# A two-layer decoder trunk: earlier loads of the second layer's operands, a mix by broadcast factors, and a gate stage that frees its banks before the exponentials

## The chip, the core and the metric

The kernel runs on one core of one Trainium2 chip. The metric is the time of one execution on the device, in microseconds (us); less is better. An execution with a hardware profile gives the trace on which everything below rests. TensorE is called PE, VectorE DVE, ScalarE ACT, GpSimd POOL; SP is SyncE, which here only issues DMA transfers. PEld is TensorE's loading of weights.

## The reference, cut to what matters

A trunk of two residual layers over 2048 tokens of width 1024. Both layers project the normalised input, compute a mixer output of 768 columns and a memory attention of 256 columns (4 heads against 256 memory tokens), multiply both by a gate and project back:

```python
for i in range(2):
    h = rmsnorm(x, norm_w[i])
    mix, q_mem, gate = gla_mixer(...) if i == 0 else dilated_mixer(...)
    mem_o = memory_attention(q_mem, mem_n, w_memkv[i])
    branch = concatenate([mix, mem_o], axis=-1) * silu(gate)
    x = x + branch @ w_out[i]
return rmsnorm(x, final_norm_w)

def dilated_mixer(h, w_in):          # 6 heads of 128 columns
    for g, (window, dil) in enumerate(((128, 1), (512, 4), (2048, 16))):
        q, k, v = split((h @ w_in[:, g's columns]))
        o, lse = dilated_group(rope(q), rope(k), v, window, dil)
    wts = softmax(stack(lses), axis=0)     # over the three groups
    o = einsum('gbth,gbthd->bthd', wts, stack(outs))
    q_mem, gate = split(h @ w_in[:, the rest], [256])
```

Everything is float32 at the interface. The kernel multiplies in float16 with a high and a low part of each operand, three matmuls for one product.

## The kernel before, in words

**Layer 1** (0 to about 982 us) is gated linear attention in two passes. The second pass walks over 16 blocks of 128 tokens in pairs (m, m + 8): queries, gate, memory attention, output projection (`a2_out`, 24 matmuls of 128x256 for each quarter), the norm of the next layer (`a2_norm`), and for each pair `a2_pair`.

**The seven products.** Layer 2 projects by a fast matrix multiplication: a 2x2 split of a product into seven products instead of eight. Its left operands, sums and differences of quarters of the normalised input, are made by `a2_pair`: `put` (near L880) splits one operand into a high and a low float16 part, SP transposes it by DMA (L890), and it stays in SBUF (operands 0 to 4 of the first half of the tokens, pool h2p) or is stored to DRAM (L892, nine tensors h2d) to be loaded later. Layer 2 uses the operands in the order `OPS = (0, 4, 1, 5, 3, 2, 6)`. `load_h2` (L1013 to 1027) loads the nine stored ones at the start of layer 2: operands 5 and 6 of the first half into wo0 and wo1, then all seven of the second half into wo2, wo3 and the pool wp. They are 128 x 4096 float16, 1 MB each.

**A half.** `sw_half` (L1040) computes 1024 tokens of 256 columns of a projection as seven products of 48 matmuls of 128x128 into two banks ps_mm and one ps_x. A product waits for its weight operand and its input operand; after it, `snap` copies, L1085 adds on DVE and a `fin` given by the caller uses the result. The bank is given back (`rel`) by the `fin` of its last product.

**Weights.** `weights` makes seven operands of a set of 256 columns: a raw 1 MB load into the single buffer stg (L974), per operand one ACT copy (L990) and one DVE step for the low part (L992), and four POOL subtractions (L998). The operands live in eight buffers wq.

**Order of the work.** From layer 2 on, the order on every engine is decided while the program is built. Each piece of work is a Python generator that yields an engine with an estimated time, a wait for an event or a semaphore; a planner (`Flow`) plays them against each other, and instructions are emitted in the order in which the planner lets them go. A changed estimate or condition therefore moves instructions on all engines. On the chip, each engine runs its instructions strictly in that order.

**The mix.** `combos` (L1572 to 1670) does the softmax-weighted sum over the three groups. It runs three times, for a pair of heads each: twice amid layer 2 (near 1600 to 1760 and 2040 to 2160 us) and once in the gate stage. There are 24 items of 128x512 in each run, and each item costs four DVE operations of 128x128 with a per-token scalar: L1655 for the first group of a sum, L1657 for the two that are added to it.

**The gate stage** (`last_stage`, L1779; 2319 to 2580 us) computes the gate's four sets of 256 columns in two halves each, and the second layer's memory attention between them. `gate_fin` takes a result from the bank or from a copy cx: the stored mix is fetched (L1807), the exponent's argument is made on DVE (L1818) or POOL (L1821), ACT does exp, ln and exp (L1824, L1826, L1828), POOL multiplies by the mix or by the memory output OM (L1832, L1835), and DVE multiplies by the gate's own input (L1844), which is the step that frees the bank. The result goes to DRAM (brd). The sets run as (set, half) = (0,0), (0,1), (1,0), (1,1), (3,0), (2,0), (2,1), (3,1); the weights of set 3 are made twice.

**The rows** (`Rows`, L2033 to 2150; from 2580 us) are the output projection of 16 blocks: load the branch row (L2081, L2083), find its scale (L2094), split it on ACT and DVE (L2101, L2103), transpose it by DMA (L2108), then twice 24 matmuls of 128x512 against the output weights (split on ACT and DVE at L2063, L2065), add, normalise (L2132 to L2147) and store. Before, the weights and the first rows are brought in while the last two gate halves run.

## Time and profile before

| what | us |
|---|---|
| median of 3 runs | 2759.14 |
| lowest and highest | 2752.9, 2767.9 |
| the profiled execution | 2755.03 |
| its span in the trace | 2753.0 |
| mean granted clock of TensorE | 0.96 |
| TensorE busy in 0 to 550 (layer 1, first pass) | 483.73 |
| in 550 to 982 (layer 1, second pass) | 401.12 |
| in 1110 to 2319 (layer 2 up to the gate) | 1145.52 of 1209 |

The rows of the other stretches stand in the prediction. In such a table of windows, each engine has its busy microseconds and, in brackets, its instructions; PEclk is the share of TensorE's full clock that was granted while it worked, and DMA the mean busy share of the 16 DMA engines. A row of waits reads: engine, what the waiting instruction writes, its line, then after the arrow the engine that released it with what it wrote and the line, then the sum in us, how many, the longest. A row of groups reads: line, engine, operation, output and input with their tile names, shape, count; then busy us and the mean ns of one; then the engine's idle us ahead of them with what ended it. A row of a timeline has start, duration and the instruction. Matmuls are pipelined: the spacing of their starts tells their cost.

### The profile page before, as it was taken

To read this page: it belongs to the slowest core of one execution; us is meant where nothing else is said; L and a number is where in the kernel's file an instruction comes from. 1 tells how busy PE (TensorE), PEld (TensorE's weight loads), DVE (VectorE), ACT (ScalarE), POOL (GpSimd) and SP (SyncE) were. 2 spreads that over 40 slices of the span, in tenths; PEclk is the share of its full clock that TensorE was granted. 3 is DMA by queue.
4 is the path that set the end of the run, shared out by engine and by line. 5 is a ranking of instruction groups with operands and counts; after the bars stand their busy time and mean duration, and the time that the engine had idled before them with its cause. 6 is when DMAs were issued, how large, how long until landed. Compare 5 with 4: busy or idle time off the path is not lost. (4 is left out here: it accounts for less than half of the span.)

```text
span 2753.0 us, 58869 instructions
## 1 busy us (share of the span) xinstructions
PE 2491.2 (90%) x23431; PEld 1906.5 (69%) x23431; DVE 1718.0 (62%) x3515; ACT 1339.5 (49%) x2938; POOL 865.6 (31%) x712
## 2 busy tenths in 40 slices
PE   6999889899999857989999899999999997877898
PEld 5888778788888755475858484758484767877544
DVE  6445654565666543656665688666787663888654
ACT  6355654553444333445555454555554554656422
POOL 0000000021112122545453444553545443756300
PEclk9999999999999988999999999999999998988899
DMA  5244892455556764676777789776798767678774
GB/s 191 74 130 147 278 271 85 155 117 120 123 137 159 156 152 160 142 157 168 157 170 154 152 196 227 159 165 152 172 207 215 155 151 162 160 190 209 195 207 126
DMA packets 729495, 454.53 MB, mean 165 GB/s; under 512 B 386514, under 2 KB 677892, under 8 KB 728068
## 3 DMA queue, kind: packets, MB, share of 16 engines
q1 hardware_dynamic: 609412, 421.27, 56.3%
q10 hardware_dynamic: 119808, 29.51, 9.5%
q8 instruction: 183, 3.00, 0.5%
q14 instruction: 92, 0.75, 0.1%
HBM read 246.82 MB, written 134.51 MB: 139 GB/s over the span
## 5 line engine op out<-in xcount | busy, mean ns | idle before, releaser
L275 PE MATMUL ps_mm<-w,hT 128*128 128x256 f16 (+1 forms) x1408 | 393.6, 280 | 23.5 <-ACT v L625 11.6
L276 PE MATMUL ps_mm<-w,hT 128*128 128x256 f16 (+1 forms) x1408 | 392.3, 279 | 0.0
L277 PE MATMUL ps_mm<-w,hT 128*128 128x256 f16 (+1 forms) x1408 | 391.4, 279 | 0.4 <-DVE hT L517 0.4
L277 PEld LDWEIGHTS <-w 128*128 128x128 f16 x2080 | 220.5, 106 | 122.9 <-issue 11.5
L276 PEld LDWEIGHTS <-w 128*128 128x128 f16 x2080 | 220.9, 106 | 112.2 <-issue 16.8
L275 PEld LDWEIGHTS <-w 128*128 128x128 f16 x2080 | 221.0, 106 | 106.4 <-DMA w<-h2d 6.1
L275 PE MATMUL ps_mm<-w,w 128*128 128x128 f16 (+1 forms) x1172 | 262.5, 260 | 6.4 <-ACT p L1069 3.0
L1075 POOL TENSOR_TENSOR u<-u,p 128x512 f32<-128x512 f32 x128 | 176.0, 1375 | 290.1 <-ACT u L1069 284.1
L276 PE MATMUL ps_mm<-w,w 128*128 128x128 f16 (+1 forms) x1172 | 261.8, 259 | 1.3 <-DVE w L992 1.3
L277 PE MATMUL ps_mm<-w,w 128*128 128x128 f16 (+1 forms) x1172 | 261.5, 259 | 0.0
L269 POOL TENSOR_TENSOR stg<-mp,stg 128x512 f16<-128x512 f32 x16 | 18.5, 1156 | 728.9 <-ACT stg L268 725.0
L992 DVE SCALAR_TENSOR_TENSOR w<-stg,wsc,w 128x512 f16<-128x512 f32 x217 | 192.0, 885 | 70.6 <-ACT w L990 70.3
L1471 ACT ACTIVATE pm<-pm,st,qsc 128x256 f32<-128x256 f32 (+1 forms) x288 | 156.9, 545 | 114.9 <-DVE st L1465 103.6
L998 POOL TENSOR_TENSOR stg<-stg 128x512 f32<-128x512 f32 x124 | 170.6, 1376 | 121.9 <-DVE w L992 109.0
L1479 POOL TENSOR_TENSOR ph<-pm,ph 128x512 f16<-128x512 f32 (+2 forms) x144 | 155.7, 1082 | 160.0 <-ACT ph L1477 72.4
L990 ACT ACTIVATE w<-stg,wsc 128x512 f16<-128x512 f32 x217 | 154.3, 714 | 97.3 <-POOL stg L998 26.3
L275 PE MATMUL ps_mm<-w,h 128*128 128x128 f16 x896 | 162.9, 227 | 19.3 <-ACT w L990 11.6
L276 PE MATMUL ps_mm<-w,h 128*128 128x128 f16 x896 | 162.6, 226 | 13.5 <-DVE w L992 13.5
L276 PEld LDWEIGHTS <-hT 128*128 128x128 f16 x1408 | 141.3, 100 | 44.8 <-issue 24.7
L1191 ACT ACTIVATE hl<-cx 128x512 f16<-128x512 f32 x126 | 79.1, 628 | 183.4 <-DVE cx L1085 94.0
L1085 DVE TENSOR_TENSOR cx<-ps_x,u 128x512 f32<-128x512 f32 x128 | 88.0, 688 | 119.8 <-PE ps_x L277 102.6
L277 PE MATMUL ps_mm<-w,h 128*128 128x128 f16 x896 | 162.5, 226 | 0.0
(439 smaller groups left out, 7949.9 us busy)
## 6 DMA issues: line engine op xcount, KB each, us to landing
stg<-in_w_in_b SPq DMA_DIRECT2D x62, 512.0 KB
qkd<-hl SPq DMA_DIRECT2D x144, 192.0 KB
stg<-in_w_in_b SPq DMA_DIRECT2D x72, 256.0 KB
vud<-hl SPq DMA_DIRECT2D x72, 256.0 KB
q<-qkd SPq DMA_DIRECT2D x72, 256.0 KB
od<-cx SPq DMA_DIRECT2D x72, 256.0 KB
fo<-od SPq DMA_DIRECT2D x72, 256.0 KB
x<-in_x SPq DMA_DIRECT2D x32, 512.0 KB
```

Of the source, the lines that this page charges most:

```text
L269: G.tensor_tensor(out=lo, in0=src, in1=hi, op=ALU.subtract)
L275: PE.matmul(o, sh, mh, start=first, stop=False, skip_group_check=free)
L276: PE.matmul(o, sh, ml, start=False, stop=False, skip_group_check=free)
L277: PE.matmul(o, sl, mh, start=False, stop=last, skip_group_check=free)
L990: A.activation(out=t[:, 0], in_=src, func=AF.Copy, scale=s1)
L992: V.scalar_tensor_tensor(out=t[:, 1], in0=src, scalar=s1, in1=t[:, 0], op0=ALU.mult, op1=ALU.subtract)
L998: G.tensor_tensor(out=o_, in0=i0, in1=i1, op=ALU.subtract)
L1075: G.tensor_tensor(out=d, in0=d, in1=sn["p1"], op=ALU.add)
L1085: V.tensor_tensor(out=cv(o), in0=vw(t), in1=cv(sn[tag]), op=ALU.add)
L1191: A.activation(out=hi, in_=src, func=AF.Copy, scale=SQ)
L1471: A.activation(out=p_, in_=p_, func=AF.Exp, scale=sc, bias=st[:, sj[jj]:sj[jj] + 1], accum_out=st[:, 16 + sj[jj]:17 + sj[jj]])
L1479: G.tensor_tensor(out=ph[:, width:2 * width], in0=pm[:, :width], in1=ph[:, :width], op=ALU.subtract)
```

## The change

- **Operands.** h2p now holds operands 0, 4, 1, 5, 3 of the first half, in the order of use. In the last block of layer 1, three of the second half (0, 4, 1) are loaded for 384 of 512 tokens into the wp pool ahead of the block's memory attention, and after the block's output projection operands 2 and 6 of the first half go whole into wo0 and wo1, and 5 and 3 of the second half for 384 tokens into wo2 and wo3. The last pair's transposes fill the remaining 128 tokens in place. `load_h2` is left with operands 2 and 6 of the second half. `a2_norm` writes a tile of its own rather than over its input.
- **Mix.** An item is one 128x512 multiply by factors that are read with a broadcast, on DVE or POOL, whichever has less planned work, and, for two of three groups, one 128x512 add on DVE. In the order that comes out, 25 multiplies stand on DVE (9, 9 and 7 in the three runs) and 47 on POOL (15, 15, 17), with 48 adds on DVE.
- **Gate stage.** The mix or memory output is fetched ahead by a thread of its own; the memory output goes through DRAM (omd). DVE makes the exponent's argument always (now L1845), then multiplies the gate's input into the fetched tile (L1849) and gives the bank back; exp, ln, exp (L1854 to 1858) and POOL's multiply follow. Four weight sets instead of five, the last with six tiles outside wq (three of gx, three of wq2); the halves run (0,0), (0,1), (1,0), (1,1), (2,0), (3,0), (2,1), (3,1).
- **Rows.** They are set up at the start of the gate stage; their weights go into the h2p tiles as the last half-0 products free them, and raw weights and the first two rows into stg and h2_0. The tiles have 256 columns each, so a row is 2 x 48 matmuls of 128x256 rather than 2 x 24 of 128x512. The third row and later ones load into wp, after the last half. All 56 gate products now stand ahead of the first row on TensorE.

The diff, cut to what the text speaks of:

```diff
-    for o in range(5):
-        h2s[0][o] = tl(h2p, [P, 2, 4, 512], F16, f"h2_{o}")
+    OPS = (0, 4, 1, 5, 3, 2, 6)
+    DIRECT, EARLY = (0, 4, 1, 5, 3), (0, 4, 1)
+    for n_, o in enumerate(DIRECT):
+        h2s[0][o] = tl(h2p, [P, 2, 4, 512], F16, f"h2_{n_}")
...
-            V.scalar_tensor_tensor(out=xt, in0=xt, scalar=r, in1=nw1, op0=ALU.mult, op1=ALU.mult)
-            return xt
+            xn = tl(kx, [P, D], F32, "x")
+            V.scalar_tensor_tensor(out=xn, in0=xt, scalar=r, in1=nw1, op0=ALU.mult, op1=ALU.mult)
+            return xn
+
+        def early(o, pl, tag):
+            t = h2s[1][o] = tl(pl, [P, 2, 4, 512], F16, tag)
+            SY.dma_start(t.rearrange("p a k t -> p (a k) t")[:, :, 0:384],
+                         h2_d[o].rearrange("p a k t -> p (a k) t")[:, :, 0:384])
...
             if n == NB - 1:
                 raw0 = load_raw(0, wp, "w")
                 raw1 = load_raw(NJ, wp, "w")
+                for o in EARLY:
+                    early(o, wp, "w")
...
-            xns.append(a2_norm(a2_out(b, bT, it)))
+            xt = a2_out(b, bT, it)
+            if n == NB - 1:
+                for o in (2, 6):
+                    h2s[0][o] = tl(wo01, [P, 2, 4, 512], F16, f"wo{o == 6:d}")
+                    SY.dma_start(h2s[0][o], h2_d[7 + (o == 6)])
+                for o in (5, 3):
+                    early(o, wo23, f"wo{2 + (o == 3)}")
+            xns.append(a2_norm(xt))
...
-        for o in (5, 6):
...
-        yield "t", 12.0
-        for o in OPS:
-            if o in (2, 6):
-                yield "w", raw_free[o == 6]
-            h2s[1][o] = tl(wo23, [P, 2, 4, 512], F16, f"wo{o - 1}") if o in (3, 4) else \
-                tl(wp, [P, 2, 4, 512], F16, "w")
+        for o in (2, 6):
+            yield "w", raw_free[o == 6]
+            h2s[1][o] = tl(wp, [P, 2, 4, 512], F16, "w")
...
-            yield "V", 0.9
-            for f in range(4):
-                fs = slice(f * P, (f + 1) * P)
-                sc_ = F_[:, g * 32 + i * 16 + c * 4 + f:g * 32 + i * 16 + c * 4 + f + 1]
-                if g == 2:
-                    V.tensor_scalar(out=og[:, fs], in0=og[:, fs], scalar1=sc_, scalar2=None, op0=ALU.mult)
-                else:
-                    V.scalar_tensor_tensor(out=acc[:, fs], in0=og[:, fs], scalar=sc_, in1=acc[:, fs], op0=ALU.mult,
-                                           op1=ALU.add)
+            at = g * 32 + i * 16 + c * 4
+            fb = F_[:, at:at + 4].unsqueeze(2).to_broadcast([P, 4, P])
+            o4 = og.rearrange("p (f d) -> p f d", f=4)
+            on_v = fl.load("V") < fl.load("G")
+            yield ("V", 0.85) if on_v else ("G", 1.45)
+            (V if on_v else G).tensor_tensor(out=o4, in0=o4, in1=fb, op=ALU.mult)
+            if g < 2:
+                yield "t", 0.1
+                yield "V", 0.85
+                V.tensor_tensor(out=acc, in0=og, in1=acc, op=ALU.add)
...
+            def fetch(c, ni):
+                yield "w", e_acc[n * 2 + ni][c] if n < 3 else e_OM[c]
+                yield "g", s_gf
+                oc = tl(gb, [P, 512], F32, "fo")
+                yield "S", 0.5
+                if n < 3:
+                    SY.dma_start(oc, acc_d[n * 2 + ni][c])
+                else:
+                    SY.dma_start(oc.rearrange("p (f d) -> p f d", f=4), om_d[c][:, :, ni * P:(ni + 1) * P])
...
+            for ci, ni in ((0, 0), (1, 1), (1, 0), (0, 1)):
+                outs[ni, hf + 2 * ci] = (Ev(), [])
+                fl.spawn(fetch(hf + 2 * ci, ni), 1)
...
             def fin(src, ci, ni, ps, rel):
                 c = hf + 2 * ci
...
                 yield "g", s_e
                 e = tl(ge, [P, 512], F32, "e")
-                if ps or fl.load("V") <= fl.load("G"):
-                    yield "V", 0.65
-                    V.tensor_scalar(out=e, in0=src, scalar1=neg, scalar2=87.0, op0=ALU.mult, op1=ALU.min)
-                else:
-                    yield "G", 1.35
-                    G.tensor_scalar(out=e, in0=src, scalar1=neg, scalar2=87.0, op0=ALU.mult, op1=ALU.min)
+                yield "V", 0.65
+                V.tensor_scalar(out=e, in0=src, scalar1=neg, scalar2=87.0, op0=ALU.mult, op1=ALU.min)
+                yield "w", outs[ni, c][0]
+                oc = outs[ni, c][1][0]
+                yield "V", 0.8
+                V.scalar_tensor_tensor(out=oc, in0=src, scalar=minv if n == 3 else inv, in1=oc, op0=ALU.mult,
+                                       op1=ALU.mult)
                 yield "t", 0.1
+                fl.put(rel)
                 yield "A", 0.6
                 A.activation(out=e, in_=e, func=AF.Exp)
                 yield "A", 0.7
                 A.activation(out=e, in_=e, func=AF.Ln, bias=one1)
                 yield "A", 0.6
                 A.activation(out=e, in_=e, func=AF.Exp, scale=-1.0)
-                yield "w", there
                 yield "G", 1.4
...
+                G.tensor_tensor(out=e, in0=e, in1=oc, op=ALU.mult)
...
-        for m, n, hf, rel in ((0, 0, 0, False), (0, 0, 1, True), (1, 1, 0, False), (1, 1, 1, True), (2, 3, 0, True),
-                              (3, 2, 0, False), (3, 2, 1, True), (4, 3, 1, True)):
...
+        for n, hf in ((0, 0), (0, 1), (1, 0), (1, 1), (2, 0), (3, 0), (2, 1), (3, 1)):
+            yield from sw_half(W[n], hf, False, 1, False, gate_fin(n, hf), late_jobs)
...
-            for q in range(KT):
-                mm3(t, bT[:, 0, q, :], bT[:, 1, q, :], w[:, 0, q, :], w[:, 1, q, :], q == 0, q == KT - 1)
+            for i in range(2):
+                w = self.w[2 * j + i]
+                for q in range(KT):
+                    mm3(t[:, i * 256:(i + 1) * 256], bT[:, 0, q, :], bT[:, 1, q, :], w[:, 0, q, :], w[:, 1, q, :],
+                        q == 0, q == KT - 1)
```

Three places of the order. The first is SP at the end of layer 1 and the start of layer 2: h2d0 to h2d6 are the stored operands 0 to 6 of the second half, h2d7 and h2d8 the two of the first half; wo, w and tq are tiles, stg is the raw projection weight, vud a store of values, x1d a store of the residual. Before:

```order
L890 DMA_TRANSPOSE tq_1596_11409<-stg_1587_11370 128x8x128
L892 DMA h2d6_86_174<-tq_1596_11409 1024x1x128
L1160 DMA mw_1597_11451<-in_mw 128x256
L954 DMA wo0_1599_11455<-h2d7_87_175 128x4096
L954 DMA wo1_1604_11517<-h2d8_88_176 128x4096
L954 DMA vud0_0_125_213<-hl_1610_11629 256x1x512
L974 DMA stg_1617_11795<-in_w_in_b 128x8x128 x2
L954 DMA vud0_1_126_214<-hl_1616_11791 256x1x512
L954 DMA rope0_1621_11855<-in_rope 128x1024
L954 DMA vud0_0_125_213<-hl_1619_11850 256x1x512
L954 DMA w_1625_11878<-h2d0_80_168 128x4096
```

After, the end of layer 1:

```order
L881 DMA w_1595_11257<-h2d4_84_172 128x8x384
L881 DMA w_1596_11259<-h2d1_81_169 128x8x384
L901 DMA h2d6_86_174<-tq_1555_10895 1024x1x128
L870 DMA x1d_37_125<-x_1585_11134 128x1024
L270 DMA_TRANSPOSE mpt_1572_10978<-stg_1573_10981 128x8x128
L861 DMA x_1602_11282<-in_x 128x1024
L896 DMA_TRANSPOSE w_1594_11255<-stg_1613_11403 128x8x128
L896 DMA_TRANSPOSE w_1596_11259<-stg_1613_11403 128x8x128
L943 DMA wo0_1605_11387<-h2d7_87_175 128x4096
L881 DMA wo2_1607_11391<-h2d5_85_173 128x8x384
L943 DMA wo1_1606_11389<-h2d8_88_176 128x4096
L881 DMA wo3_1608_11393<-h2d3_83_171 128x8x384
```

And after, the start of layer 2:

```order
L901 DMA h2d6_86_174<-tq_1618_11433 1024x1x128
L1175 DMA mw_1619_11475<-in_mw 128x256
L973 DMA vud0_0_125_213<-hl_1630_11649 256x1x512
L973 DMA w_1634_11758<-h2d2_82_170 128x4096
L994 DMA stg_1638_11817<-in_w_in_b 128x8x128 x2
L973 DMA vud0_1_126_214<-hl_1637_11813 256x1x512
```

The loads of h2d7 and h2d8 have moved ahead of most of the last pair's transposes, those of operands 4, 1, 5 and 3 of the second half stand in layer 1 with 384 of 512 tokens, ahead of or behind the memory attention's transpose (mpt), and between the first store of vud and the raw weight there is now one whole operand (h2d2) where there was none.

The second is POOL in the first mix: u is an addition for a projection, ph the low part of softmax results that a transpose waits for, stg a subtraction for weight operands, fo an item of the mix and fac its factors. Before:

```order
L1075 TENSOR_TENSOR u_2579_19388<-u_2579_19388,p_2575_19322 128x512
L1075 TENSOR_TENSOR u_2592_19537<-u_2592_19537,p_2575_19322 128x512
L1479 TENSOR_TENSOR ph_19542<-pm_19427,ph_19542 128x512
L998 TENSOR_TENSOR stg_19328<-stg_19328 128x4x128 x2
L1479 TENSOR_TENSOR ph_19694<-pm_19581,ph_19694 128x512
L998 TENSOR_TENSOR stg_19328<-stg_19328 128x4x128
```

After, the same place:

```order
L1494 TENSOR_TENSOR ph_19542<-pm_19429,ph_19542 128x512
L1018 TENSOR_TENSOR stg_19337<-stg_19337 128x4x128 x2
L1494 TENSOR_TENSOR ph_19695<-pm_19583,ph_19695 128x512
L1670 TENSOR_TENSOR fo_19545<-fo_19545,fac_19088 128x512
L1670 TENSOR_TENSOR fo_19689<-fo_19689,fac_19088 128x512
L1018 TENSOR_TENSOR stg_19337<-stg_19337 128x4x128
L1670 TENSOR_TENSOR fo_19786<-fo_19786,fac_19088 128x512
L1086 TENSOR_TENSOR u_2637_19899<-u_2637_19899,p_2627_19773 128x512
```

Three multiplies of the mix stand between the softmax results and the weights, where before only u, ph and stg took turns.

The third is DVE at the end of the gate stage: bh is the low part of a row's operand with the ACT scale stok, cx a result copied out of its bank, e the gate's argument or product, gm, p2e, itok and cj the steps to a row's scale. Before:

```order
L199 RECIPROCAL stok_34192<-itok_34193 128x1
L2097 TENSOR_SCALAR cj_34194<-winv_5408,itok_34193 128x2
L1844 SCALAR_TENSOR_TENSOR e_33912<-cx_33704,winv_5408,e_33912 128x512
L992 SCALAR_TENSOR_TENSOR w_34037<-stg_33071,wsc_5407,w_34037 128x512
L1818 TENSOR_SCALAR e_34214<-cx_34188,wneg_5411 128x512
L2103 SCALAR_TENSOR_TENSOR bh_34211<-bx_34043,stok_34192,bh_34211 128x1024
L1844 SCALAR_TENSOR_TENSOR e_34196<-cx_34177,cols_88,e_34196 128x512
L1085 TENSOR_TENSOR cx_34300<-ps_x_34069,u_4247_33910 128x512
L1818 TENSOR_SCALAR e_34302<-cx_34300,wneg_5411 128x512
L1844 SCALAR_TENSOR_TENSOR e_34214<-cx_34188,cols_88,e_34214 128x512
L1844 SCALAR_TENSOR_TENSOR e_34302<-cx_34300,cols_88,e_34302 128x512
```

After, where bh is written into half of the tile wo:

```order
L1096 TENSOR_TENSOR cx_34079<-ps_mm_33736,p_4277_33787 128x512
L195 TENSOR_SCALAR p2e_34081<-gm_34023 128x1
L196 TENSOR_SCALAR p2e_34081<-p2e_34081 128x1
L198 TENSOR_SCALAR itok_34025<-p2e_34081 128x1
L199 RECIPROCAL stok_34024<-itok_34025 128x1
L2118 TENSOR_SCALAR cj_34026<-winv_5412,itok_34025 128x2
L1096 TENSOR_TENSOR cx_34089<-ps_x_33915,u_4279_33846 128x512
L1845 TENSOR_SCALAR e_34087<-ps_mm_33677,wneg_5415 128x512
L2124 SCALAR_TENSOR_TENSOR wo_4236_33147<-stg_33854,stok_34024,wo_4236_33147 128x1024
```

Before, the low part of a row (L2103) stood ahead of the last gate result (cx_34300); after, the first row's low part (L2124) stands behind the last product's result (cx_34089) and a gate step.

146 lines of the change are left out of this document (68 added, 78 removed).

## The prediction

> **What bounds the kernel now.** I read the page first, then a table of engine time by stretch, then the waits of TensorE in the stretches that the change touches.
>
> ```profile
> span 2753.0 us, 58869 instructions
> PE 2491.2 (90%) x23431; PEld 1906.5 (69%) x23431; DVE 1718.0 (62%) x3515; ACT 1339.5 (49%) x2938; POOL 865.6 (31%) x712
> ```
>
> TensorE is busy for 90% of the span, so everything that can be won without removing products lies in the other 262 us, and in matmuls that run at a lower clock. The change removes no product. The question is therefore where those 262 us sit.
>
> ```profile
> core 0: us, PE busy (x) PEld busy (x) DVE busy (x) ACT busy (x) POOL busy (x), PEclk, DMA share, GB/s
> 982.00:1110.00 128.00, 87.87 (x858) 64.62 (x858) 54.01 (x65) 40.50 (x66) 42.93 (x34) 0.84 0.53 155
> 1600.00:1760.00 160.00, 149.28 (x1517) 104.96 (x1515) 137.12 (x283) 78.39 (x168) 74.78 (x62) 0.98 0.84 200
> 2040.00:2160.00 120.00, 107.89 (x853) 64.76 (x851) 92.91 (x214) 56.98 (x123) 56.09 (x47) 0.97 0.86 197
> 2319.00:2580.00 261.00, 207.37 (x3144) 201.09 (x3142) 198.34 (x348) 155.93 (x332) 164.66 (x111) 0.87 0.72 179
> 2580.00:2745.00 165.00, 165.00 (x767) 74.78 (x765) 87.62 (x148) 42.75 (x77) 1.27 (x1) 1.00 0.65 183
> ```
>
> The five stretches are the start of layer 2, the two mixes inside it, the gate stage and the output rows. TensorE is idle for 40 us in the first, 11 and 12 us in the mixes and 54 us in the gate stage; the granted clock falls only in the first (0.84) and in the gate stage (0.87). The rows are full: 165 of 165 us at clock 1.00, with nothing to win.
>
> **Term A, the start of layer 2.** These are TensorE's waits from 982 to 1110 us, longest first:
>
> ```profile
> PE ps_mm L275 <- DMA wo<-h2d: 11.9, 1, 11.9
> PE ps_x L275 <- DMA wo<-h2d: 9.7, 1, 9.7
> PE ps_mm L275 <- ACT w L990: 8.9, 2, 8.1
> PE ps_x L275 <- DMA w<-h2d: 6.0, 1, 6.0
> ```
>
> Three of the four wait for an operand tile. Each such gap costs a second time, as the matmuls before and after the longest show:
>
> ```profile
> 1000.07 0.22 PE L275 MATMUL ps_mm<-w,h 128*128 128x128 f16 x1
> 1003.03 0.22 PE L277 MATMUL ps_mm<-w,h 128*128 128x128 f16 x1
> 1015.19 0.29 PE L275 MATMUL ps_mm<-w,wo 128*128 128x128 f16 x1 [11.95 <-DMA wo<-h2d]
> 1020.12 0.22 PE L275 MATMUL ps_x<-w,h 128*128 128x128 f16 x1
> ```
>
> Ahead of the gap 53 matmul steps take 2.96 us, 0.056 each, so a product of 48 takes 2.7 us. The 48 behind the gap, from 1015.19 to 1020.12, take 4.9 us: 2.2 us more. Three gaps hold 11.9 + 9.7 + 6.0 = 27.6 us and about 3 x 2.2 = 6.7 us of slow matmuls.
>
> The change loads operands 2 and 6 of the first half before the last pair of blocks is written out, and five of the second half go partly or wholly into place in layer 1. What is late next is the first projection weight: its load now stands behind one 1 MB operand load on SP's queue (the order above). The price of that is read from the issue of the two loads that were late:
>
> ```profile
> 1008.87 1.03 SPq L954 DMA_DIRECT2D wo<-h2d  x2
> ```
>
> The two megabytes had landed by 1015.19, 6.3 us after the issue: 3.2 us for one. Term A is -27.6 - 6.7 + 3.2 = **-31 us**. At best all 40 us of idleness go; at worst only the longest wait goes, with its slow product (-14).
>
> **Term B, layer 1's end.** The three early loads (0.75 MB each) stand on SP ahead of the last memory attention's transposes. By the 3.2 us per megabyte they are worth at most 2.25 x 3.2 = 7 us of lateness. Against it, 24 output matmuls stand ahead of that attention (2.6 us of cover by the 0.109 us spacing under term S). From -2.6 to +7, I take **+3**, since SP's order is strict there. The separate tile for the norm only frees a wait of VectorE; I count it as nothing, hidden by TensorE's own work.
>
> **Term M, the first two mixes.** The waits of TensorE in the first mix (1600 to 1760), then in the second (2040 to 2160):
>
> ```profile
> PE ps_o L1511 <- DMA pt<-ph: 5.3, 3, 2.4
> PE ps_o L1511 <- DVE cx L1526: 4.1, 1, 4.1
> ...
> ```
>
> ```profile
> PE ps_o L1511 <- DMA pt<-ph: 6.4, 5, 4.0
> PE ps_o L1511 <- DVE cx L1526: 4.7, 1, 4.7
> ```
>
> So of 23 us idle, 4.1 + 4.7 = 8.8 are waits for a VectorE eviction, 11.7 wait for transposes. The mix's own prices: POOL's nearest multiply over the whole trace, VectorE's nearest 128x512 operation, the shortest, median and longest of the small mix operation, and the small operations of the third mix (2316 to 2580):
>
> ```profile
> L1075 POOL TENSOR_TENSOR u<-u,p 128x512 f32<-128x512 f32 x128 | 176.0, 1375 | 290.1 <-ACT u L1069 284.1 <-DVE mden L1965 4.0 <-DMA qkd<-hl 1.9
> L1267 DVE TENSOR_TENSOR xr<-xr,cx 128x512 f32<-128x512 f32 x36 | 34.7, 964 | 10.8 <-POOL cx L1263 9.5
> L1657 DVE SCALAR_TENSOR_TENSOR fo<-fo,fac,fo x192: 332/343/1710, 1608.7 to 2498.5; 128x128 f32<-128x128 f32 x192
> L1657 DVE SCALAR_TENSOR_TENSOR fo<-fo,fac,fo 128x128 f32<-128x128 f32 x64 | 34.1, 591 | 4.2 <-DMA fo<-od 4.1
> L1655 DVE TENSOR_SCALAR fo<-fo,fac 128x128 f32<-128x128 f32 x32 | 21.4, 727 | 4.7 <-DMA fo<-od 4.7
> ```
>
> One mix costs VectorE 34.1 + 21.4 = 55.5 us today. After, 9 multiplies and 16 adds of 128x512 stand on VectorE in each of the first two, 25 x 0.964 = 24 us, and 15 multiplies on POOL, 15 x 1.375 = 21 us. So VectorE is freed of some 31 us a mix, and its 8.8 us of waits go; the 11.7 us of transposes stay, eased at most a little. No row shows a broadcast multiply, so the bounds are -23 (all idleness goes) and +41 (each of the 30 POOL multiplies, standing between softmax operations in POOL's order, delays TensorE by its full 1.375). POOL is busy for under half of both stretches, so I take **-10**.
>
> The small operation has a median of 343 ns and a longest of 1710: VectorE is being held up by something. The Trainium skill, page "SBUF — State Buffer", section "Who interferes with whom", says that a VectorE instruction with two SBUF inputs contends with a GpSimd instruction that reads SBUF, and that the later one blocks fully; the trace's spread agrees. By that rule the 41 us of POOL multiplies could hold VectorE's adds as long, and M would be about 0, the sum 2690.
>
> **Term C, the gate stage.** Rows of 2316 to 2580 that the change touches, and TensorE's waits from 2310 to 2600:
>
> ```profile
> L1821 POOL TENSOR_SCALAR e<-cx,wneg 128x512 f32<-128x512 f32 x15 | 34.9, 2329 | 10.1 <-DVE cx L1085 6.2 <-DVE w L992 3.6 <-DMA brd<-e 0.3
> L992 DVE SCALAR_TENSOR_TENSOR w<-stg,wsc,w 128x512 f16<-128x512 f32 x28 | 25.6, 914 | 11.8 <-ACT w L990 11.8
> L998 POOL TENSOR_TENSOR stg<-stg 128x512 f32<-128x512 f32 x16 | 24.1, 1507 | 19.6 <-DVE w L992 19.2
> L1818 DVE TENSOR_SCALAR e<-cx,wneg 128x512 f32<-128x512 f32 x8 | 4.8, 614 | 0.1
> ```
>
> ```profile
> PE ps_mm L276 <- DVE w L992: 15.4, 4, 8.4
> PE ps_mm L275 <- ACT w L990: 7.7, 3, 3.7
> PE ps_mm L275 <- DVE e L1844: 7.6, 2, 5.8
> PE ps_x L276 <- DVE w L992: 5.4, 1, 5.4
> ```
>
> 28.5 us wait for weight operands, and 7.6 for the gate product (L1844) that frees a bank. The change makes four weight sets instead of five, gives the last one further tiles, and multiplies out of the bank before the exponentials rather than after POOL's multiply, so that a bank no longer waits for ACT and POOL. VectorE's work becomes 198.3 - 55.5 (third mix) + 23 x 0.964 = 22.2 (7 multiplies, 16 adds) - 7 x 0.914 = 6.4 (one set fewer) + 15 x 0.614 = 9.2 (POOL's first step, moved over): 168 us. POOL's becomes 164.7 - 34.9 - 4 x 1.507 + 17 x 1.375 = 147. TensorE's is 207.4 x 0.87 = 180 at full clock. The memory output's detour through DRAM adds 16 stores of 128 KB and 8 loads of 256 KB to SP's queue, 4 MB or 13 us by the price under A, asked for a half ahead and so hidden by the products of that half; the output weights' splits lie in this stage already. No engine fills 261 us. VectorE, through which every chain passes, reached 77% in the second mix (92.9 of 120) and 86% in the first (137.1 of 160); 168 us at these shares are 218 and 195. I take 79%, nearer to the present 76%: 212 us, **-49**. The low end is TensorE's 180 at the first mix's 93%: 194. The high end drops only the bank wait, a fifth of the weight waits (5.7) and 7.6 us of slow matmuls behind them: 240.
>
> **Term G, the gap before the first row.** Before, the operands of the first rows were split ahead of the last gate steps, and rows followed products without a gap. Now the low half of row 0 stands on VectorE behind the last product's eviction and one gate step (the order above). How long a transposed operand takes from there:
>
> ```profile
> 2590.88 1.28 DVE L2103 SCALAR_TENSOR_TENSOR bh<-stg,stok,bh 128x1024 f16<-128x1024 f32 x1
> ```
>
> ```profile
> 2596.63 1.15 ACT L2101 ACTIVATE bh<-w,stok 128x1024 f16<-128x1024 f32 x1 [3.92 <-DMA bT<-bh]
> ```
>
> From the end of the split (2592.16) to the tile being free again behind its transpose (2596.63) is 4.5 us. Eviction and gate step are two VectorE operations of about 0.7, so 1.4 + 1.3 + 4.5 = 7.2 us, and the slow clock behind it about 2.2: **+9**. It is 0 if gate steps of an earlier half leave VectorE free sooner, and some 25 if three rows in turn pay the 7.2.
>
> **Term S, the rows' shape.** The 768 matmuls of 128x512 become 1536 of 128x256. The trace has that shape in layer 1's output:
>
> ```profile
> 960.75 0.27 PE L275 MATMUL ps_x<-wo,bT 128*128 128x256 f16 x1
> ...
> 962.93 0.27 PE L277 MATMUL ps_x<-wo,bT 128*128 128x256 f16 x1
> L276 PEld LDWEIGHTS <-bT 128*128 128x128 f16 x768 | 75.8, 99 | 41.4 <-issue 5.1
> ```
>
> Twenty steps take 2.18 us: 0.109. 1536 x 0.109 = 167.4 against 165: **+3**, rounded up, with each 99 ns weight load hidden behind the matmul before.
>
> **Sum.** -31 + 3 - 10 - 49 + 9 + 3 = -75. The profiled execution took 2755.0 us (its span 2753.0), 0.15% under the median of 2759.1; so 2755 - 75 = 2680.
>
> **Rivals.**
> *The gate stage stays bound by its weights.* The waits for w are the largest there and one load buffer still feeds all sets. With 240 us, C is -21: 2708.
> *Everything fits.* Gate stage 195 us and no gap (C -66, G 0): 2654. For it, no engine is over 168 us; against it, the order of the rows.
> *The early loads only collide elsewhere*, so that the change doesn't do what it says at layer 2's start: A -14, B +7, 2701. For it: 2.25 MB ahead of transposes on one queue; against it: 432 us of layer 1 in which to spread them.
> *POOL's multiplies delay the softmax.* M at +41 and the third mix's 17 x 1.375 = 23 on top: 2680 + 51 + 23 = 2754, no change. Against it: POOL's 47% in the mixes.
> *Slower: weight loads no longer hide.* If a 256-column matmul doesn't cover the load for the next, a step is 0.109 + 0.099 and the rows take 1536 x 0.208 = 319 us, S +154: 2831. It decides as soon as the spacing exceeds 0.2 us. Against it stand the twenty steps at 0.109 with a load each. The Trainium skill, page "TensorE: Matmul & The Clock Gate", section "What overlaps and what doesn't", has a weight load overlap matmuls in flight only when the row group differs, which speaks for this rival; the 0.109 us spacing disagrees.
>
> **How the numbers follow.** My forecast gets 0.47, the weights rival 0.17, everything fits 0.13, the collision 0.12, POOL's delay 0.07, the slow rows 0.04. A measurement of this kernel can tell about 0.5% (14 us) from no change. All cases but the last two are faster by more: 0.89, same 0.07, slower 0.04. The range has to leave out those two and reach the others with their bounds: below, 2654 less a further 9 from A's best end and 10 from M's (2635); above, 2708 with the collision's 21 together (2729).
>
> **What would show it.** Right: no wait for an operand from 982 to 1110 and a clock near 1; an eviction wait gone in both mixes; a gate stage of 195 to 220 us with its bank wait gone; one gap of 5 to 12 us before row 0; steps of 0.109 in the rows. Wrong: weight waits of 25 us and more left in the gate stage, POOL's multiplies as what softmax waits for, steps beyond 0.109, or several gaps among the rows.

## The result, and the profile after

The changed kernel took 2738.3 us in the median of 7 runs (2731.7 to 2745.0), the kernel before 2759.1 (2752.9 to 2769.9): a ratio of 0.992, 95% interval 0.9894 to 0.9946. It is faster by 21 us, and 75 were forecast. Its profiled execution, at 2745.0, is the slowest of its seven, and that of before near its fastest, so the two traces lie only 10 us apart: they show where time was won and lost, but their sum is 11 us short of the medians.

The page of the changed kernel, first lines:

```profile
span 2743.0 us, 60361 instructions
PE 2485.6 (91%) x24199; PEld 1971.5 (72%) x24199; DVE 1695.7 (62%) x3308; ACT 1336.4 (49%) x2931; POOL 896.8 (33%) x740
```

The same five stretches, moved to where they lie now:

```profile
core 0: us, PE busy (x) PEld busy (x) DVE busy (x) ACT busy (x) POOL busy (x), PEclk, DMA share, GB/s
982.00:1110.00 128.00, 113.20 (x1041) 76.39 (x1042) 67.81 (x95) 49.01 (x83) 51.71 (x41) 0.93 0.49 141
1578.00:1740.00 162.00, 146.49 (x1432) 101.53 (x1430) 121.47 (x208) 75.78 (x162) 93.60 (x73) 0.96 0.88 192
2028.00:2160.00 132.00, 117.95 (x1015) 74.24 (x1013) 98.73 (x171) 62.54 (x134) 80.83 (x63) 0.97 0.86 196
2315.00:2566.00 251.00, 197.07 (x3145) 193.14 (x3143) 181.25 (x282) 148.71 (x321) 143.20 (x107) 0.89 0.74 190
2566.00:2736.00 170.00, 169.57 (x1536) 151.04 (x1536) 88.97 (x150) 45.61 (x81) 2.53 (x2) 0.99 0.65 186
```

The start of layer 2 is repaired: 15 us idle instead of 40. The mixes are not: VectorE's busy share fell, yet TensorE is idle for 16 and 14 us there, more than before. The gate stage is nowhere near 212 us. POOL's work there fell about as reckoned (143 us, 147 forecast), VectorE's by 17 us to 181, where 168 were forecast.

Such windows can't say what was lost where, because the work has moved in time. The eviction of a product into cx (L1085 before, L1096 after) can: both kernels do 192 of them, and up to the gate stage (number 169) in the same order of products; behind it two of the halves have changed places, and only the first and the last point compare. The table gives when the numbered ones start in the trace of before, and how much earlier (-) or later each kernel is there, in us. The last four columns are experiments that are told below.

| point | before | changed | early_only | mix_old | mix_ghost | third_cut |
|---|---|---|---|---|---|---|
| first product of layer 2 | 982.5 | +13.5 | +5.4 | +3.6 | +2.2 | +7.1 |
| eviction 25 | 1215.0 | -22.7 | -33.0 | -36.9 | -38.4 | -27.6 |
| 73, ahead of the first mix | 1570.6 | -21.8 | -32.9 | -37.9 | -41.1 | -27.9 |
| 103, behind it | 1809.1 | -13.1 | -34.0 | -37.4 | -37.5 | -18.8 |
| 133, ahead of the second mix | 2030.4 | -12.6 | -29.7 | -34.5 | -35.5 | -17.6 |
| 163, behind it | 2267.2 | -2.5 | -26.7 | -33.3 | -29.8 | -8.1 |
| 169, gate stage begun | 2339.7 | -4.5 | -26.3 | -30.7 | -29.5 | -10.8 |
| 192, last one | 2579.7 | -21.2 | -25.6 | -43.2 | -52.4 | -57.6 |
| last row's end | 2745.6 | -10.0 | -25.3 | -32.8 | -41.4 | -44.9 |

Down the changed column: 13.5 lost ahead of layer 2, 36.2 won at its start, 19.3 lost from eviction 73 to 163, 16.7 won in the gate stage, 11.2 lost at the rows. Of the 13.5, 7.1 are there already at 573 us (the first norm step, L872), where nothing that was changed has run. Without these 7 the change is worth 17 us in the trace.

TensorE's waits at the start of layer 2:

```profile
PE ps_mm L275 <- ACT w L1010: 9.1, 2, 8.2
PE ps_tr L262 <- DVE sg L845: 1.9, 1, 1.9
```

No operand is waited for; the wait for the first weights, 8.9 us before, has stayed at 9.1. For the mixes, the same work has to be compared, so these are TensorE's waits from eviction 73 to eviction 163, before (1571 to 2267):

```profile
PE ps_o L1511 <- DMA pt<-ph: 21.1, 14, 4.0
PE ps_o L1511 <- DVE cx L1526: 8.9, 2, 4.7
...
```

and after (1549 to 2265):

```profile
PE ps_o L1526 <- DMA pt<-ph: 42.3, 21, 5.8
PE ps_tr L1561 <- ACT pm L1486: 2.3, 2, 1.2
...
```

The waits for a VectorE eviction (8.9 us) are gone, and the waits for transposed softmax tiles have doubled, from 21.1 to 42.3 us. The busy times of the same two stretches:

```profile
1571.00:2267.00 696.00, 661.66 (x6521) 456.85 (x6519) 511.37 (x1090) 355.34 (x776) 335.39 (x283) 0.99 0.78 180
1549.00:2265.00 716.00, 668.28 (x6540) 460.98 (x6539) 502.36 (x950) 356.03 (x774) 382.66 (x313) 0.98 0.81 176
```

So of the 19.3 us lost there, TensorE's idle time holds 13 (34 to 48) and slower matmuls hold 6 (662 to 668 us busy for the same products). And VectorE (the third figure) was freed of 9 us in all, not of 31 a mix. The mix's own steps on it did become cheaper, from 62.8 + 30.4 to 35.8 + 20.1 us:

```profile
L1657 DVE SCALAR_TENSOR_TENSOR fo<-fo,fac,fo 128x128 f32<-128x128 f32 x128 | 62.8, 554 | 2.8 <-DMA fo<-od 2.8
L1655 DVE TENSOR_SCALAR fo<-fo,fac 128x128 f32<-128x128 f32 x64 | 30.4, 535 | 8.0 <-DMA fo<-od 8.0
L1674 DVE TENSOR_TENSOR fo<-fo,fo 128x512 f32<-128x512 f32 x32 | 35.8, 1118 | 7.7 <-POOL fo L1670 7.5
L1670 DVE TENSOR_TENSOR fo<-fo,fac 128x512 f32<-128x512 f32 x18 | 20.1, 1115 | 9.5 <-DMA fo<-od 9.5
```

but its other operations got longer by 28 us, the 104 weight steps for one from 90.7 to 100.4. In the gate stage (2290 to 2570):

```profile
PE ps_mm L275 <- ACT w L1010: 16.6, 2, 11.5
...
PE ps_mm L276 <- DVE w L1012: 9.8, 4, 5.6
PE ps_g L275 <- DMA wo<-wo: 7.4, 1, 7.4
PE ps_mm L275 <- ACT fo L1010: 7.0, 1, 7.0
PE ps_x L276 <- DVE w L1012: 6.4, 1, 6.4
```

The bank wait (7.6 us for L1844) is gone, as meant, but the waits for weight operands are 39.8 us instead of 28.5 (fo is a weight operand here, in a tile shared with the third mix). The 7.4 is the gap ahead of row 0.

### The profile page after: what moved, and what is told of

Read it like the earlier page. It is cut to its first block, busy times and chain, and to the rows that moved or that the text cites. A ratio compares the mean times of both kernels' runs of the same rounds, so it can differ in the third digit from the quotient of the medians.

```text
span 2743.0 us, 60361 instructions
## 1 busy us (share of the span) xinstructions
PE 2485.6 (91%) x24199; PEld 1971.5 (72%) x24199; DVE 1695.7 (62%) x3308; ACT 1336.4 (49%) x2931; POOL 896.8 (33%) x740
## 5 line engine op out<-in xcount | busy, mean ns | idle before, releaser
L275 PE MATMUL ps_mm<-w,hT 128*128 128x256 f16 (+1 forms) x1408 | 393.5, 280 | 24.6 <-ACT v L626 13.4
L275 PE MATMUL ps_mm<-w,w 128*128 128x128 f16 (+1 forms) x1140 | 254.6, 260 | 2.6 <-ACT p L1080 2.6
L276 PE MATMUL ps_mm<-w,w 128*128 128x128 f16 (+1 forms) x1140 | 254.2, 259 | 0.0
L277 PE MATMUL ps_mm<-w,w 128*128 128x128 f16 (+1 forms) x1140 | 254.0, 259 | 0.0
L275 PE MATMUL ps_mm<-w,h 128*128 128x128 f16 x848 | 154.0, 227 | 25.6 <-ACT w L1010 25.6
L276 PEld LDWEIGHTS <-hT 128*128 128x128 f16 x1408 | 141.3, 100 | 45.9 <-issue 25.6
L1010 ACT ACTIVATE w<-stg,wsc 128x512 f16<-128x512 f32 x207 | 147.1, 713 | 52.1 <-issue 24.0
L276 PE MATMUL ps_mm<-w,h 128*128 128x128 f16 x848 | 153.6, 226 | 11.6 <-DVE w L1012 11.6
L275 PEld LDWEIGHTS <-wo 128*128 128x128 f16 x1408 | 150.9, 107 | 13.9 <-DMA wo<-wo 7.6
L277 PEld LDWEIGHTS <-wo 128*128 128x128 f16 x1408 | 150.8, 107 | 12.6 <-issue 6.5
```

Source lines behind the costliest of these rows:

```text
L275: PE.matmul(o, sh, mh, start=first, stop=False, skip_group_check=free)
L276: PE.matmul(o, sh, ml, start=False, stop=False, skip_group_check=free)
L277: PE.matmul(o, sl, mh, start=False, stop=last, skip_group_check=free)
L1010: A.activation(out=t[:, 0], in_=src, func=AF.Copy, scale=s1)
```

## The experiments

All times are medians beside runs of the kernel before on the same chip, whose own median lay between 2754.5 and 2759.9; the ratio to it stands with its interval. Each trace is of one execution.

**early_only.** The kernel before with the first part alone (tile order, early loads, norm into a tile of its own); its diff is the first part of the diff above.

> The kernel before with the early operand loads alone (order of the tiles, loads in layer 1, a tile of its own for the norm); mix, gate stage and rows as before. Theory: the loads at the start of layer 2 were worth what the trace of the changed kernel shows there, 36 us won after the boundary less 5 lost ahead of it, and nothing of it is given back later: 2759 - 30 = about 2729, ratio 0.989. Rival: the loads move the planner's order and the gain is eaten later by the mixes even without the new mix, as the trace of the changed kernel shows it eaten (2745 to 2755, ratio 0.995 to 0.999).

2727.4 us, ratio 0.9895 (0.9864 to 0.9925), runs from 2723.6 to 2730.9. That part alone is faster than the whole change, whose fastest run took 2731.7. Its column stays at -34 to -25 from eviction 25 to the end: the gain isn't given back by the old mix and the old gate stage. By the medians the rest of the change costs 11 us. The traces lie 15 us apart, and 8 of these are there at the first product of layer 2 (+5.4 and +13.5), up to which both kernels run the same instructions; so not all of the 11 can be laid on the new mix and gate stage.

**mix_old.** The changed kernel with the old mix.

```diff
-            (V if on_v else G).tensor_tensor(out=o4, in0=o4, in1=fb, op=ALU.mult)
...
-                V.tensor_tensor(out=acc, in0=og, in1=acc, op=ALU.add)
+            yield "V", 0.9
+            for f in range(4):
...
+                    V.tensor_scalar(out=og[:, fs], in0=og[:, fs], scalar1=sc_, scalar2=None, op0=ALU.mult)
```

> The changed kernel with the mix's four small VectorE operations per item put back in all three runs of the mix; all else as changed. Theory A (POOL, in its strict order, waits for the mix's loads and stands ahead of the softmax's low parts, so their transposes come late): the 18 to 20 us that the changed kernel lost over the two mixes come back, about 2738 - 18 = 2720, and the waits of TensorE for transposed softmax tiles in the mixes fall from 31 us to about 12, while waits for a VectorE eviction of some 9 us return. Theory B (transposes are late because the DMA engines are fuller, whoever multiplies): 2738 or slower.

2722.8 us, ratio 0.9884 (0.9852 to 0.9915). 15.5 us come back by the medians. In the trace, 4.6 instead of 19.3 us are lost from eviction 73 to 163, and TensorE's waits for transposes there are 23.5 us instead of 42.3. The new mix costs time: the three other kernels here that keep the new mix as it is lose 19.1 to 25.1 us in that stretch, the four others with the old one 0.7 to 7.3.

**mix_dve.** All broadcast multiplies on VectorE.

```diff
-            on_v = fl.load("V") < fl.load("G")
+            on_v = True
```

> The changed kernel with all 72 broadcast multiplies on VectorE, none on POOL. VectorE then has 24 multiplies and 16 adds in a mix, 40 x 0.75 = 30 us against 55 before. Theory A (POOL's head-of-line wait): waits for transposed softmax tiles fall back to about 12 us in the two mixes without the VectorE waits of before, 2738 - 25 = about 2713. Theory B (DMA): no change, 2735 to 2742. Theory C (VectorE is the scarce engine, so the share on POOL helps): slower than the changed kernel, 2745 to 2755.

2726.8 us, ratio 0.9898 (0.9861 to 0.9935): within the interval of mix_old, and between the figures of theories A and B. From eviction 73 to 163 it loses 3.4 us, with 26.3 us of waits for transposes. So it is the share on POOL that hurts. Against the old mix it gains nothing, and it doesn't free VectorE either: VectorE is busy for 518 us in that stretch, 513 in mix_old and 502 in the changed kernel. The broadcast multiply's median is 742 ns in the changed kernel and the small operation's 343 before, which looks like half the cost for an item; but the means are 1109 and 566.

**mix_late.** In the first two mixes the planner is told that loads land later.

```diff
-            yield "t", 2.5
+            yield "t", 5.5 if hp < 2 else 2.5
```

> The changed kernel, but the planner is told for the first two mixes that a mix item's load lands 3 us later, so that multiplies stand further back in the orders of POOL and VectorE; as many multiplies stay on POOL. Theory A1 (POOL loses its time by waiting, in its strict order, for a load that is not there yet): most of the 20 us that the two mixes lost come back, 2738 - 12 = about 2726, and POOL's idle time ahead of the multiplies falls from 16 us in each of the two mixes to under 5. Theory A2 (POOL loses it by the multiplies themselves, 14 x 1.2 us a mix, and by the port that it shares with VectorE): no change, 2733 to 2743.

2738.8 us, ratio 0.9938 (0.9917 to 0.9959): no change. In each of the two mixes 13 multiplies stand on POOL instead of 15. The multiplies on POOL in the first mix, in the changed kernel (1545 to 1750):

```profile
L1670 POOL TENSOR_TENSOR fo<-fo,fac 128x512 f32<-128x512 f32 x15 | 18.2, 1211 | 17.9 <-DMA fo<-od 17.6
```

and with the later loads (1570 to 1765):

```profile
L1670 POOL TENSOR_TENSOR fo<-fo,fac 128x512 f32<-128x512 f32 x13 | 15.3, 1178 | 4.8 <-DMA fo<-od 3.3 <-issue 1.5
```

POOL's 17.6 us of waiting for loads, which looked like the cause, shrank to 3.3, and TensorE's wait for transposes there is still 15.2. From eviction 73 to 163 this kernel loses 13.4 us instead of 19.3, but not as little as mix_old.

**mix_fill.** Two fills in place of each multiply on POOL, with the product left out.

```diff
-            (V if on_v else G).tensor_tensor(out=o4, in0=o4, in1=fb, op=ALU.mult)
+            if on_v:
+                V.tensor_tensor(out=o4, in0=o4, in1=fb, op=ALU.mult)
+            else:
+                G.memset(og, 0.5)
+                G.memset(og, 0.5)
```

> The changed kernel, with each multiply of the mix that the planner puts on POOL replaced by two fills of the same tile with a constant, which write SBUF and read nothing (the product is left out, so these items hold a constant). Theory A2-time (POOL's occupation, and with it the place of softmax's low parts behind it, costs the 10 us a mix): 2733 to 2743 if the two fills last about as long as one multiply (1.2 us). Theory A2-port (a POOL operation that reads SBUF and VectorE's operations with two SBUF inputs hold each other up, so that both chains get longer): VectorE's weight step (L1012) in the first mix goes back from 1017 ns to about 870, the add from 1091 to under 850, and the time to about 2728.

2726.9 us, ratio 0.9889 (0.9873 to 0.9905). POOL and VectorE in its first mix (1532 to 1745):

```profile
L1674 POOL MEMSET fo<- 128x512 f32 x15 | 7.9, 526 | 0.9
L1673 POOL MEMSET fo<- 128x512 f32 x15 | 7.9, 524 | 15.4 <-DMA fo<-od 15.2
```

```profile
L1012 DVE SCALAR_TENSOR_TENSOR w<-stg,wsc,w 128x512 f16<-128x512 f32 x29 | 26.5, 913 | 4.1 <-ACT w L1010 4.1
L1678 DVE TENSOR_TENSOR fo<-fo,fo 128x512 f32<-128x512 f32 x16 | 17.5, 1092 | 3.1 <-POOL fo L1674 3.0
```

Against the changed kernel's rows,

```profile
L1012 DVE SCALAR_TENSOR_TENSOR w<-stg,wsc,w 128x512 f16<-128x512 f32 x28 | 28.5, 1017 | 3.6 <-ACT w L1010 3.6
L1674 DVE TENSOR_TENSOR fo<-fo,fo 128x512 f32<-128x512 f32 x16 | 17.5, 1091 | 3.8 <-POOL fo L1670 3.7
```

the weight step got 104 ns shorter and the add none, and 18.8 us are lost from eviction 73 to 163: as much as with the multiplies. The total looks like a gain of 11 us, but in the trace it arises ahead of the mixes: the first product of layer 2 starts 1.9 us later than before, in the changed kernel 13.5, and at eviction 25 they are at -34.0 and -22.7. So the port theory doesn't explain the loss in the mixes, although the total has the figure that it named.

**mix_ghost.** The multiplies on POOL are planned but not issued, so those items lack their factor; in the trace, the instructions of TensorE, VectorE and ACT come one for one in the order of the changed kernel.

```diff
-            (V if on_v else G).tensor_tensor(out=o4, in0=o4, in1=fb, op=ALU.mult)
+            if on_v:
+                V.tensor_tensor(out=o4, in0=o4, in1=fb, op=ALU.mult)
```

> The changed kernel with the 47 multiplies of the mix that the planner puts on POOL planned but not issued (those items are added without their factor): the orders of TensorE, VectorE and ACT stay word for word as in the changed kernel, and POOL only lacks the multiplies. Theory A2-time (POOL's time for them, with softmax's low parts, the additions and the weight subtractions behind it): the stretch of the two mixes, in which the changed kernel lost 17 us, loses 7 as in the kernel before, and the time falls to 2715 to 2725. Theory P (the plan: with some multiplies on POOL the planner lets other work on TensorE go earlier than it is ready): the loss of 17 us stays, 2727 to 2738.

2719.4 us, ratio 0.9867 (0.9839 to 0.9896); its trace is that of the fastest of its four runs. From eviction 73 to 163 it loses 11.3 us: 8.0 less than the changed kernel, 6.7 more than mix_old. The same stretch in six kernels, in us:

| | before | changed | mix_fill | mix_ghost | mix_dve | mix_old |
|---|---|---|---|---|---|---|
| lost against before | 0 | 19.3 | 18.8 | 11.3 | 3.4 | 4.6 |
| TensorE idle | 34.3 | 47.7 | 45.1 | 47.4 | 36.1 | 37.3 |
| of it waiting for transposes | 21.1 | 42.3 | 40.3 | 40.0 | 26.3 | 23.5 |
| TensorE busy | 662.2 | 668.2 | 670.3 | 660.5 | 663.9 | 663.9 |
| VectorE busy | 511.9 | 502.2 | 493.3 | 484.0 | 518.4 | 513.4 |

Both theories hold in part. Without the multiplies TensorE waits for transposes as long as with them: these waits belong to the order in which the planner puts the other engines' work once it counts on POOL, which the three kernels share, and not to POOL's time. What goes with the multiplies is 8 us of TensorE's busy time, the same products in slower matmuls; fills in their place keep it, and no run shows why. Each figure is of one trace, and kernels with the same mix differ by up to 7 us in this stretch, so the split is rough.

**gate_prio.** The four gate weight sets are planned first, and the tiles shared with the mix are taken only after the mix.

```diff
+            if tag == "fo":
+                yield "w", e_mix2
...
-        for W in wsets[2:]:
+        for W in wsets[2:-4]:
             yield from weights(W)
+        fl.spawn(gate_weights(), 0)
```

> The changed kernel with the four gate weight sets planned at the highest instead of the lowest priority (and the three tiles that the last set shares with the mix taken only once the mix is done). Theory D (the weight chain, a hop between ACT, VectorE and POOL for each operand, waits behind other work on each of them, and TensorE waits 40 us for it): weight waits fall below 15 us, 2738 - 25 = about 2713. Theory E (VectorE and ACT have no more room in the gate stage): waits only move, to banks and the mix, 2733 to 2743.

2734.5 us (10 runs, 2718.9 to 2752.3), ratio 0.9908 (0.9881 to 0.9935); the trace is that of the slowest run. TensorE's longest waits from 2340 to 2575:

```profile
PE ps_mm L275 <- ACT fo L1013: 30.0, 1, 30.0
PE ps_g L275 <- DMA wo<-wo: 5.3, 1, 5.3
```

Every wait for a tile w is gone, and one wait of 30.0 us stands in their place: the last set's second operand, whose tile (fo) is free when the third mix is done. The waits only moved, but not for theory E's reason: what they moved to is the third mix.

**gate_prio_homes.** The same, with the shared tiles given to the last set's fourth, sixth and seventh product, not the second to fourth.

```diff
-        wsets[-1].home = [(s_wq, wq, "w")] + [(s_gx, gx, "fo")] * 3 + [(s_w2, wq2, "w")] * 3
+        wsets[-1].home = [(s_wq, wq, "w")] + [(s_w2, wq2, "w")] * 2 + [(s_gx, gx, "fo"), (s_w2, wq2, "w")] + [(s_gx, gx, "fo")] * 2
```

> The changed kernel, new mix, with the gate weights at the highest priority and the shared tiles used for the last three operands of the last set. Theory F (third mix as chain): the one wait of 30 us for a shared tile shrinks to about 15, 2734 - 10 = about 2724. Theory E: 2730 to 2740.

2732.3 us, ratio 0.9914 (0.9888 to 0.9939). The 30.0 us wait shrank to 17.7, and the gate stage (eviction 169 to 192) won 23.5 us against before instead of 18.1. In the total the 2 us are not beyond noise. The wait and a second one of 3.9 for such a tile end at 2490 and 2494 us, where the third mix ends (2493):

```profile
2489.66 0.27 PE L275 MATMUL ps_mm<-fo,h 128*128 128x128 f16 x1 [17.75 <-ACT fo L1013]
2493.84 0.27 PE L276 MATMUL ps_mm<-fo,h 128*128 128x128 f16 x1 [3.91 <-DVE fo L1015]
```

**third_cut.** The same, and the third mix leaves out two of its three groups.

```diff
-                 for g in (2, 1, 0)]
+                 for g in ((2, 1, 0) if hp < 2 else (2,))]
...
```

> As the run before, but the third mix leaves out two of its three groups (16 of 24 items: their loads, multiplies and adds), so that two heads of the output hold one group alone. Theory F: with both chains short the gate stage comes to some 200 us, 2738 - 35 = about 2703. Theory E (TensorE, VectorE and ACT full even so): 2720 to 2730, since only some 16 us of VectorE's and POOL's work are gone.

2709.2 us, ratio 0.9829 (0.9802 to 0.9855): 23 us under the run before. The gate stage wins 46.8 us against before, nearly the 49 forecast, though with less work than was forecast for it. Its longest waits (2340 to 2545):

```profile
PE ps_g L275 <- DMA wo<-wo: 8.3, 1, 8.3
PE ps_o L1979 <- DMA mp<-mh: 5.8, 4, 2.3
PE ps_mm L275 <- DVE fo L1861: 4.9, 1, 4.9
```

The third mix took 131 us from the start of its first operation to that of its last in the changed kernel, 144 in the run before, 59 here. It is a chain: items through three tiles, each with a load, a multiply and an add, and the gate results of set 2 and the tiles of the last set wait for its end. The 21.6 us of waits for its tiles in the run before are gone, and the stage is 23.3 us shorter. But the cut also takes work off VectorE. From eviction 169 to 192, the rows of the changed kernel, the run before, this run and mix_old_prio_homes (below):

```profile
2335.00:2559.00 224.00, 179.19 (x2884) 175.51 (x2881) 169.59 (x257) 139.39 (x304) 135.07 (x100) 0.89 0.76 196
2332.00:2549.00 217.00, 174.81 (x2882) 170.12 (x2879) 178.30 (x260) 139.04 (x302) 133.25 (x97) 0.91 0.80 205
2329.00:2522.00 193.00, 172.79 (x2879) 168.55 (x2876) 150.51 (x232) 136.41 (x301) 118.81 (x87) 0.96 0.84 201
2317.00:2533.00 216.00, 179.32 (x2890) 174.52 (x2887) 187.29 (x335) 143.13 (x311) 110.98 (x84) 0.93 0.82 206
```

VectorE has 28 us less to do here than in the run before, so this run alone doesn't part the chain from the work. The other rows speak against the work: with 187 us of it on VectorE the last kernel needs 216 us, and with 170 the changed one needs 224.

**mix_old_prio_homes.** Old mix, with both edits to the weights.

> The changed kernel with the old mix, the gate weights planned at the highest priority, and the three tiles that the last weight set shares with the mix used for its last three operands rather than for its second to fourth. Theory D+F (the gate stage waits for two chains, the weights and the third mix, which with the old mix ends 54 us earlier against the last product than with the new): 2723 - 20 = about 2703, weight waits under 10 us. Theory E (engines full): 2718 to 2725.

2717.4 us, ratio 0.9863 (0.9839 to 0.9887): 5 us under mix_old, where 20 were expected. Waits for weights are down to 1 us; 10.9 us for evictions and 10.5 for a gate product (L1860) have come up.

**order32.** As that one, set 3 ahead of set 2.

```diff
...
-        for n, hf in ((0, 0), (0, 1), (1, 0), (1, 1), (2, 0), (3, 0), (2, 1), (3, 1)):
+        for n, hf in ((0, 0), (0, 1), (1, 0), (1, 1), (3, 0), (2, 0), (3, 1), (2, 1)):
```

> The fastest kernel so far (old mix, gate weights at the highest priority, shared tiles last: 2717) with gate set 3, which needs the memory output, ahead of set 2, which needs the third mix, in both halves. Theory F (the third mix is the chain that the gate stage ends on): set 2 asks for it a half (some 19 us) later, so the 10.5 us wait for the gate product in a bank goes, 2717 - 9 = about 2708. Theory E (engines): 2714 to 2722.

2717.0 us, ratio 0.9859 (0.9843 to 0.9876): no change, and the gate product is still waited for (10.2 us). With both chains eased the next in line decides, and this run doesn't name it.

**order32_mix0.** As order32, the third mix planned first as well.

```diff
-            yield from combos(2, gx, s_gx, 1, mixed2)
+            yield from combos(2, gx, s_gx, 0, mixed2)
...
-        fl.spawn(mix2(), 1)
+        fl.spawn(mix2(), 0)
```

> As the run before, with the third mix too at the highest priority in the plan. Theory F: the mix's 128 us shrink to about 100 and the stage ends earlier, about 2700. If the mix is bound by its three tiles and the latency of its loads, not by its place in the queues: as order32, about 2708.

2712.4 us (2710.5 to 2714.3), ratio 0.9839 (0.9825 to 0.9854). The mix's last item began 37 us earlier than in order32 (2424.4 instead of 2461.2). Counted as above the mix took 110 us instead of 129; its items alone took 94 instead of 98, so it mostly began earlier rather than ran faster. The stage did not get shorter for it: from eviction 163 to the end of the last row this trace wins 10.9 us against before, that of order32 15.8. This is the lowest median of a kernel that computes everything, 45 us under before on its chip, but its interval overlaps that of order32. Its waits for the gate product have grown:

```profile
PE ps_mm L275 <- DVE fo L1860: 15.0, 3, 10.5
```

## Why the prediction was wrong, point by point

**A, start of layer 2 (-31 forecast): right.** -36.2 in the changed trace, -38.4 in that of early_only, from the first product to eviction 25, and -33.4 to -40.6 in all thirteen traces that have the early loads. The three operand waits are gone. The granted clock came to 0.93 and not near 1. The 3.2 us of lateness that the term charged for the first weights did not come: that wait is as long as before.

**B, end of layer 1 (+3): right.** +13.5 less the 7.1 that were there before any changed instruction is 6.4, inside -2.6 to +7. All thirteen kernels with the early loads run the same instructions up to here, and the same difference is -2.0 to +9.0 in their traces, with a median of 2.5; a single trace could have fallen at either end. The 7.1 themselves are in no term.

**M, the first two mixes (-10 forecast, +19.3 measured): wrong, in sign.** Two steps failed. The first is "VectorE is freed of some 31 us a mix", taken as time for TensorE. VectorE was freed of 9 us in both mixes together, because its other operations took 28 us more while the mix's took 37 less; and where it was freed most, in mix_ghost (484 us busy instead of 512), TensorE lost 11.3 us all the same. The second is "the 11.7 us of transposes stay, eased at most a little": over the same work these waits went from 21.1 to 42.3 us. mix_dve and mix_old bring them back to 26.3 and 23.5, so planning a share of the mix on POOL is the cause; mix_ghost keeps them at 40.0 with no multiply executed there, so it is the changed order of the other engines that makes them, a price for which the prediction had no term. Valuing POOL's part at next to nothing because POOL was busy for under half asked the wrong question. Which moved instruction does it is open. A further 8 us, in slower matmuls, go with the multiplies themselves. "POOL's multiplies delay the softmax" was the nearest rival: the waits that it named are those that grew, but not for the reason that it gave, and its price was 51 us over the forecast for the first two mixes, against 29 measured. The rule of the Trainium skill, page "SBUF — State Buffer", section "Who interferes with whom", that an instruction of VectorE with two SBUF inputs and a GpSimd one that reads SBUF hold each other up, agrees with the 104 ns that the weight step got shorter under mix_fill, not with the add's 1091 and 1092 ns, and decides nothing here: with fills, which read nothing, 18.8 us were lost all the same.

**C, the gate stage (-49 forecast, -16.7 measured): wrong in size.** The step that failed is "168 us at these shares are 218 and 195": it took the stage to be as long as VectorE's work at a good share. The work was mis-sized by some 13 us (181), but the share is what fails: 170 us of VectorE's work took 224 us here, 187 took 216 in mix_old_prio_homes. The bank wait went as reckoned. In its place TensorE waited for two chains: the weights, which queue behind other work on three engines (39.8 us of waits), and behind them the third mix, which holds tiles and results. gate_prio moved the wait from the first to the second, and only third_cut, with both short, reached -46.8; that it also has less work is said above. Kernels with the same code for the gates won between 12.5 and 23.0 us there (mix_old and mix_ghost), so the 16.7 itself is known to a few us. The rival "the gate stage stays bound by its weights" (C at -21) had the size right and named the first of the two chains.

**G and S (+9 and +3 forecast): right.** The last gate product and the rows' first and last matmuls:

```profile
2558.26 0.22 PE L277 MATMUL ps_x<-w,w 128*128 128x128 f16 x1
2565.91 0.39 PE L275 MATMUL ps_g<-h,wo 128*128 128x256 f16 x1 [7.43 <-DMA wo<-wo]
...
2735.30 0.27 PE L277 MATMUL ps_g<-h,wo 128*128 128x256 f16 x1
```

The gap is 7.4 us (7.2 forecast), and 1536 matmuls take 169.4 us from the first start to the last, 0.110 each with the slow start. Both terms together lost 11.2 us from the last eviction to the last row's end (12 forecast). A step of 0.110 us has no room for a weight load of 99 ns beside a matmul of 0.109: the loads stay hidden, and the slower rival didn't happen. The sentence of the Trainium skill, page "TensorE: Matmul & The Clock Gate", under "What overlaps and what doesn't", that a weight load overlaps matmuls in flight only when the row group differs, doesn't hold for these.

**The sum.** In the traces A and B came to -30 (without the 7.1; -28 forecast) and G and S to +11 (+12 forecast); C and M hold the miss, 32 us and 29 us.

## What to carry to other kernels

An engine's busy share says how much work fits, not how long a stage is: ask for each stage which chain of dependent steps, through how few tiles, ends last, and price that. Work moved to an idle engine is not free: under a planner it moves the instructions of the other engines too, and here the longer waits came with that order and not with the moved work. Compare stretches with the same work in them, and means rather than medians where an operation is often held up. And undo each part alone before believing the sum: here the first part of the change alone was faster than the whole.

## What the runs showed of the hardware

POOL's 128x512 multiply by broadcast factors took 1032 to 1588 ns with a mean of 1214 in the changed kernel, less than the mean of 1375 of its addition of the same shape before, and a fill of 128x512 took 525 in the first mix of mix_fill.

VectorE's operations in one and the same order, from eviction 73 to 163, kept it busy for 502 us with 30 multiplies on POOL, 493 with 60 fills in their place and 484 with neither.

The step that starts at 573.2 us in the kernel before started 6.5 to 7.8 us later in the profiles of the five kernels that issue broadcast multiplies on POOL, and -0.3 to +4.4 us later in the eight that don't, though no mix runs ahead of 1520 us in any of them. By the first product of layer 2 the two groups are at +7.1 to +16.8 and +1.9 to +9.3 us, and this is part of what mix_old, mix_dve, mix_fill and mix_ghost seem to win. Each is one execution, and nothing here tells why; it stays open.
